# A ninth block pair by seven products, and the low parts of four down-projection weights made early and kept in DRAM

## The chip, the cores and the metric

The kernel runs on one core of one Trainium2 chip. TensorE (PE in the profile) multiplies matrices into PSUM, VectorE (DVE), ScalarE (ACT) and GpSimd (POOL) work on vectors, SyncE (SP) issues most of the transfers; ACT and POOL have transfer queues of their own. The metric is the time of one execution on the device, in microseconds, as the median of several runs.

## The reference, cut to what matters

One layer of a streaming encoder on 512 tokens of 1024 channels: four parallel token mixers with sigmoid gates and an output projection, a cross-attention into 256 memory tokens, and a gated MLP with a short causal convolution. The change touches the last gated mixer branch and the MLP:

```python
hf = _rms_norm(x, norm_ffn_pre[l])
u = _dwconv_causal(hf @ w_up[l], ffn_dw[l]) + ffn_dw_b[l]
u_g, u_v = jnp.split(u, 2, axis=-1)
yff = (jax.nn.silu(u_g) * u_v) @ w_down[l]
x = x + _rms_norm(yff, norm_ffn_post[l])
```

`w_up` is 1024 x 5632 (the first 2816 columns are the gate, the others the value), `w_down` is 2816 x 1024. Everything is float32.

## The kernel before, in words

**Number format.** A float32 matrix is held as a high part (a cast to the matmul type float32r) and a low part (the rest), and a product is three matmuls: high by high, high by low and low by high (`mm3`, line 245 in `matmul`). The split of a weight is a cast on ACT and a subtraction on DVE (`split_weights`, lines 202 and 203; `split_to`, lines 1673 and 1674). A weight of [128, 1024] is loaded into a raw tile (two of tag `wr`), split into a high and a low tile, and these come from four places each in turn (`weights_tile`, tags `wh0` to `wh3` and `wl0` to `wl3`). A new weight can be written into a place once every matmul on the weight four before it is done.

**Order.** All stages are one stream of jobs (`run_blocks`): a job has a load and split, done up to three jobs ahead, and a body with the matmuls. An entry without weights (`then`) only runs its body in its turn. The order within each engine is then settled by a planner of the tile framework: it runs through the instructions with durations of its own and takes, on each engine, what is ready there, with the program's order as priority. Semaphores hold the order between engines on the chip.

**The mixer's last branch** (`last_branch_jobs`): for the forgetting attention, eight gate blocks and four branch blocks, twelve weights of 512 KB, each with 24 matmuls of 512 columns. The output projection of the mixer comes next, by seven products in place of eight on half blocks (`SEVEN`), with sums of weights formed earlier and stored in DRAM (`Sums`).

**The up-projection** (`up_jobs`). The 22 blocks of 128 channels of gate and value are made block by block. Blocks 0 to 3 are plain. A plain block half is 24 matmuls of 512 columns. From block 5 on, every second block takes gate and value together as a 2 by 2 product of half blocks, by seven products of 12 matmuls of 256 columns each (`seven`), and the block before it is plain and laid between the products. These pairs go from 5 to 19 in the kernel before; blocks 20 and 21 are plain. In a pair, the bodies are: `a` (two products, weight: the gate block), `b` (two products, weight `z.s`, a sum of quarter blocks), `c` (one product, weight: the changed value block), `d` (one, weight `z.t`, half as wide) and `end` (one, again the weight of `c`). Between them stand the plain block's gate half (after `a`), the first half of its value (after `b`) and the second half of its value (after `d`, `second_half`, which still reads the weight fetched for the first). The sums of weights are made by POOL (lines 1755 to 1759). The sums of activations over the tokens' halves, which the products `b`, `c` and `end` read, are made once per call by `token_sums` on POOL (lines 1663 and 1665) and split into `tokh` and `tokl` (`token_split`). After the products, `done` adds the bias on ACT (line 1697) and the convolution's other taps on DVE (line 627), which frees the PSUM bank.

Beside this, in the pairs, POOL forms sums of `w_down` for the next stage (`ns.sums`, lines 575 to 578), and DVE forms sums of the activations of each pair of blocks (`down_sums`, lines 1684 to 1686).

**The down-projection** (`down_jobs`) again goes by seven products, on 11 pairs of blocks in two phases; phase 0 has two weights per pair, with 12 matmuls of 512 columns each (products M1 and M6, then M5 and M7). Its raw weights come on SP's queue (line 594) into `dw` tiles, three ahead, and are split by `split_to`. The products keep their sums in PSUM; the banks are named by tags `sc`, `tr`, `mm` and `av`, two banks each. Before, M1, M6, M5 and M7 had `sc`, `tr`, `mm` and `av`.

Of the kernel before, what the change touches and what calls it, by code (L numbers as in the profile page):

```python
# [25 lines left out]
P = 128  # L26
# [60 lines left out]
def hybrid_layer(ctx: ExitStack, tc: tile.TileContext, a: dict, out: bass.AP):  # L87
# [520 lines left out]
    def seven_banks(phase):  # L608
        names = (("M2", "sc"), ("M3", "tr"), ("M4", "mm")) if phase else (("M1", "sc"), ("M6", "tr"), ("M5", "mm"),
                                                                         ("M7", "av"))  # L610
        return {name: [bank(tag) for _ in range(2)] for name, tag in names}
# [756 lines left out]
    def last_branch_jobs():  # L1368
        yield then(open_last_branch)
        gf = gate_blocks(1, "f", mix_place, mix_done)  # L1370
        yield next(gf)
        yield next(gf)
        yield share("mm", "av")
        yield from gf
# [264 lines left out]
    def open_ffn():  # L1639
# [27 lines left out]
    def token_split(i):  # L1667
        hi, lo = ns.tok
        A.copy(hi[:, i], ns.quart[i - 4])
        V.tensor_tensor(lo[:, i], ns.quart[i - 4], hi.bitcast(F32)[:, i], ALU.subtract)  # L1670
# [17 lines left out]
    def up_jobs():  # L1688
# [56 lines left out]
        def seven(j):  # L1745
# [28 lines left out]
            def summed(i):  # L1774
                return [lambda k, h=h: h[:, i, k] for h in ns.tok]
# [39 lines left out]
        def early_places():  # L1815
            ns.pair_sums = []
            down_places(f"qa{NF // 2 - 1}", 2)

# [7 lines left out]
        pairs = {j: seven(j) for j in range(5, NF - 2, 2)}  # L1826
# [6 lines left out]
        for q, j in enumerate(pairs, EARLY - 1):  # L1833
# [37 lines left out]

        yield then(late_places)
        yield plain(NF - 2, 0, sums_of(3))
        yield plain(NF - 2, 1, sums_of(4))
# [239 lines left out]
```

## Time and profile before

| | |
|---|---|
| median of 3 runs | 1033.58 us (1033.11 to 1033.93) |
| profiled execution | 1035.12 us, of it span 1033.3 us |
| PE busy | 1024.4 us (99%), 5477 matmuls |
| DVE busy | 864.0 us (84%) |
| ACT busy | 534.4 us (52%) |
| POOL busy | 263.5 us (26%) |
| mean granted TensorE clock | 0.999 |

The span runs from the first to the last instruction of the profiled execution, and its own time is 1.8 us longer. A busy PE is one with a matmul in flight; the ends of matmuls are modelled and overlap, so the distance between starts is the better measure of a matmul's price. In a row of the chain or of the timeline the first number is the start in us from the span's start and the second the duration.

In the span, the mixer's last branch lies at about 497 to 562 us, the mixer's output from there to about 600, the up-projection's pairs from 733 to 905, the last plain blocks from there to 921, and the down-projection from 921 to 1027.

### The profile page before, as it was taken

How to read it: one execution, taken by the hardware profiler on the slowest of the kernel's cores; microseconds unless marked ns; L12 is line 12 of the kernel's file. 1: busy time of each engine (PE TensorE's matmuls, PEld its weight loads, DVE VectorE, ACT ScalarE, POOL GpSimd, SP SyncE). 2: the span in 40 equal slices, each digit the busy share in tenths (PEclk: the TensorE clock that was granted, in tenths of full speed). 3: DMA queues.
4: the chain of work that ended last, by engine and by line, in shares of the span. 5: the costliest groups of instructions: out<-in, count | busy, mean ns of one | idle time of the engine just before them, and what ended most of it. 6: DMA issues, size and time to landing. Idle time of an engine off the chain costs nothing.

```text
span 1033.3 us, 15189 instructions
## 1 busy us (share of the span) xinstructions
PE 1024.4 (99%) x5477; PEld 883.0 (85%) x5477; DVE 864.0 (84%) x1323; ACT 534.4 (52%) x893; POOL 263.5 (26%) x270
## 2 busy tenths in 40 slices
PE   9999999999999999999999999999999999999997
PEld 8888888888888988888888899999899899888886
DVE  7899999796878667888687898787989897799886
ACT  5322222376565466766543665655455455466662
POOL 4001000100011214442100031039177557226202
PEclk9999999999999999999999999999999999999999
DMA  7954344844434255767448834233456576626852
GB/s 248 317 176 106 104 147 143 280 143 115 141 102 140 63 157 137 195 184 188 154 146 264 262 123 123 82 97 116 134 164 209 180 225 210 197 81 187 274 161 82
DMA packets 194128, 169.40 MB, mean 164 GB/s; under 512 B 25295, under 2 KB 165692, under 8 KB 194053
## 3 DMA queue, kind: packets, MB, share of 16 engines
q1 hardware_dynamic: 187315, 145.08, 46.9%
q10 hardware_dynamic: 4178, 14.82, 3.9%
q0 software_dynamic: 2560, 8.54, 2.7%
q8 instruction: 43, 0.70, 0.3%
q14 instruction: 32, 0.26, 0.1%
HBM read 142.18 MB, written 26.23 MB: 163 GB/s over the span
## 4 chain that ended last, share of the span: by engine, by line
PE 95%; DVE 2%; DMA 1%; ACT 1%; issue 1%; POOL 0%; POOLq 0%; DVEq 0%; SPq 0%; ACTq 0%
PE ps_mm L245 41%; PE ps_av L245 26%; PE ps_tr L245 15%; PE ps_sc L245 11%; PE ps_tr L251 1%; PE ps_mm L463 1%; PE ps_av L463 1%; DVE e L860 0%; DMA xs<-in_x 0%; DMA ptl<-turned 0%; DVE e L1133 0%; DVE ptl L879 0%; ACT wh L202 0%; ACT e L1139 0%; DVE qk L820 0%
## 5 line engine op out<-in xcount | busy, mean ns | idle before, releaser
L202 ACT CAST wh<-wr 128x1024 fp32r<-128x1024 f32 (+1 forms) x124 | 129.5, 1046 | 188.6 <-PE ps_mm L245 70.4
L203 DVE TENSOR_TENSOR wl<-wr,wh 128x1024 fp32r<-128x1024 f32 (+1 forms) x124 | 165.3, 1334 | 30.0 <-ACT wh L202 29.5
L245 PE MATMUL ps_mm<-hth,wh 128*128 128x512 f32 (+1 forms) x472 | 173.5, 376 | 0.1
L245 PE MATMUL ps_mm<-htl,wh 128*128 128x512 f32 (+1 forms) x472 | 173.5, 376 | 0.0
L245 PE MATMUL ps_mm<-hth,wl 128*128 128x512 f32 (+1 forms) x472 | 173.2, 375 | 0.0
L245 PEld LDWEIGHTS ps_mm<-hth,wh 128*128 128x128 f32 x472 | 87.1, 188 | 15.7 <-ACT hth L164 0.3
L245 PEld LDWEIGHTS ps_mm<-hth,wl 128*128 128x128 f32 x472 | 87.0, 188 | 15.7
L245 PEld LDWEIGHTS ps_mm<-htl,wh 128*128 128x128 f32 x472 | 87.0, 188 | 15.2
L245 PE MATMUL ps_av<-htl,wh 128*128 128x512 f32 (+1 forms) x264 | 97.8, 370 | 0.0
L245 PE MATMUL ps_av<-hth,wh 128*128 128x512 f32 (+1 forms) x264 | 97.7, 370 | 0.0
L245 PE MATMUL ps_av<-hth,wl 128*128 128x512 f32 (+1 forms) x264 | 97.6, 370 | 0.0
L700 DVE SCALAR_TENSOR_TENSOR y<-y,par,y 128x508 f32<-128x508 f32 (+29 forms) x120 | 83.0, 733 | 0.0
L245 PEld LDWEIGHTS ps_av<-htl,wh 128*128 128x128 f32 x264 | 49.6, 188 | 8.1
L245 PEld LDWEIGHTS ps_av<-hth,wl 128*128 128x128 f32 x264 | 49.7, 188 | 8.0
L245 PEld LDWEIGHTS ps_av<-hth,wh 128*128 128x128 f32 x264 | 49.6, 188 | 8.0
L1673 ACT CAST wh<-dw 128x1024 fp32r<-128x1024 f32 x32 | 33.7, 1052 | 21.6 <-PE ps_av L245 8.1
L1674 DVE TENSOR_TENSOR wl<-dw,wh 128x1024 fp32r<-128x1024 f32 x32 | 39.6, 1243 | 5.5 <-ACT wh L1673 5.5
L245 PE MATMUL ps_tr<-htl,wh 128*128 128x512 f32 (+1 forms) x112 | 40.6, 363 | 0.0
L245 PE MATMUL ps_tr<-hth,wh 128*128 128x512 f32 (+1 forms) x112 | 40.6, 362 | 0.0
L245 PE MATMUL ps_tr<-hth,wl 128*128 128x512 f32 (+1 forms) x112 | 40.5, 361 | 0.0
L1920 POOL TENSOR_TENSOR qa<-qa 128x256 f32<-128x256 f32 x11 | 26.6, 2425 | 49.2 <-DVE wr L1674 25.2
L1127 POOL TENSOR_SCALAR fbias<-ck,cq 128x128 f32<-128x128 f32 (+3 forms) x32 | 21.3, 671 | 67.9 <-DVE st L1133 62.4
(558 smaller groups left out, 2739.1 us busy)
## 6 DMA issues: line engine op xcount, KB each, us to landing
wr<-in_w_in SPq DMA_DIRECT2D x38, 512.0 KB
wr<-in_w_gate SPq DMA_DIRECT2D x32, 512.0 KB
wr<-in_w_up SPq DMA_DIRECT2D x28, 512.0 KB
dw<-sums SPq DMA_DIRECT2D x44, 256.0 KB
wr<-in_w_branch SPq DMA_DIRECT2D x16, 512.0 KB
wq<-in_w_up SPq DMA_DIRECT2D x16, 512.0 KB
wp<-in_w_down ACTq DMA_DIRECT2D x14, 512.0 KB
sums<-wp ACTq DMA_DIRECT2D x14, 512.0 KB
```

The lines of the kernel that those rows point to most:

```text
L202: last_weights[:] = [order(A.copy(hi, raw[:, :n])).ins, low.tensor_tensor(lo, raw[:, :n], hi.bitcast(F32), ALU.subtract).ins]
L203: low.tensor_tensor(lo, raw[:, :n], hi.bitcast(F32), ALU.subtract).ins]
L245: steps_of[:] = [PE.matmul(ps, lhs, rhs, start=start, stop=stop, skip_group_check=again).ins]
L251: turns.append(PE.transpose(ps, x, ident[:n, :n]).ins)
L463: keep(PE.matmul(banks[c][:, :S // 2], w[p == 1][:, k, c * P:(c + 1) * P], ht[p == 2][:, i * 4 + k, :S // 2], start=(i, p, k) == (0, 0, 0) ...
L700: ins = V.scalar_tensor_tensor(dst[:, s:], src[:, :S - s], pc("conv_dw", k * 4 + j), dst[:, s:], ALU.mult, ALU.add)
L1127: G.tensor_scalar(bias[:, :w], ck[j][:, :w], -1.0, cq[:, qt, head:head + 1], ALU.mult, ALU.add)
L1673: A.copy(hi, x)
L1674: return V.tensor_tensor(lo, x, hi.bitcast(F32), ALU.subtract).ins
L1920: G.tensor_tensor(z[:, 1], z[:, 2], z[:, 1], ALU.subtract)
```

## The change

1. **Ninth pair.** The pairs go on to block 21, so blocks 20 and 21 become a pair with its plain block, as the eight before. Two plain halves (48 matmuls of 512 columns) become seven products (84 of 256).
2. **Places.** The split token sums become eight tiles of 4 KB per partition instead of two of 16 KB, so that each comes free by itself: the sums of activations for down go into four of them and into `z7` after body `c` of the last pair (`late_places`); three serve as raw tiles for down's second phase; and the last norm's gain, which was loaded as the up-projection opened, is loaded into one (`tokl3`) after the last product. The last pair of blocks has a tile of its own (`qlast`) in the place the gain had.
3. **Sums of activations.** `sums_of(2)` and `sums_of(3)` are issued after body `c` of the last pair, `sums_of(4)` after the held half of block 20, `sums_of(5)` after its last product.
4. **Banks.** In down M1, M6, M5, M7 have `mm`, `av`, `sc`, `tr` (and M2, M3, M4 have `mm`, `av`, `sc`), and the very last half product takes a `tr` bank.
5. **Low parts.** In the mixer's last branch four more jobs come after its second, fourth, eighth and tenth: each loads one of down's first four raw weights (two transfers of 256 KB on SP's queue), splits it as any weight, and stores the low part (512 KB) into a DRAM tile `lows` on POOL's queue. In down, the first four weights are cast on ACT as before, and their low parts are loaded from `lows` on POOL's queue instead of being subtracted on DVE.
6. **Start of the token sums.** A memset of one column of the first sum's tile on DVE is put behind the last norm before the MLP, and POOL's first token sum has to follow it.

```diff
     def last_branch_jobs():
         yield then(open_last_branch)
         gf = gate_blocks(1, "f", mix_place, mix_done)
-        yield next(gf)
-        yield next(gf)
-        yield share("mm", "av")
-        yield from gf
+        ns.lows = dram.tile([4 * P, D], F32R, name="lows")
+
+        def low_job(n):
+
+            def load():
+                raw = gp.tile([P, WB], F32, tag="wr", name="wr", bufs=2)[:, :D]
+                load_parts(raw, ns.sums.parts(0, n % 2, n // 2))
+                return split_weights(raw, [P, D])
+
+            return load, None, lambda hi, lo: G.dma_start(ns.lows[n * P:(n + 1) * P, :], lo) and None
+
+        for i, job in enumerate(gf):
+            if i == 2:
+                yield share("mm", "av")
+            yield job
+            if i in (1, 3, 7, 9):
+                yield low_job((1, 3, 7, 9).index(i))
...
-        ns.tok = [ns.fp.tile([P, 4, 4, S // 2], F32R, tag=n, name=n) for n in ("tokh", "tokl")]
-        ns.post = ns.fp.tile([P, D], F32, name="g_ffn")
+        ns.tok = [[ns.fp.tile([P, 4, S // 2], F32R, tag=f"{n}{i}", name=n) for i in range(4)] for n in ("tokh", "tokl")]
+        ns.last = ns.fp.tile([P, 4, S // 2], F32, name="qlast")
         ns.dw = {"dw": 1}
-        G.dma_start(ns.post, a["norm_ffn_post"][0].partition_broadcast(P))
...
+        with tc.issue_after(ns.normed[-1]):
+            V.memset(raw[0][:, 0, :1], 0.0)
...
+    def load_gain():
+        ns.post = ns.fp.tile([P, D], F32, tag="tokl3", name="g_ffn")
+        G.dma_start(ns.post, a["norm_ffn_post"][0].partition_broadcast(P))
...
-        pairs = {j: seven(j) for j in range(5, NF - 2, 2)}
+        def late_places():
+            for x in ("tokh0", "tokh1", "tokl0", "tokl1"):
+                down_places(x, 2)
+            down_places("z7", 1)
+
+        pairs = {j: seven(j) for j in range(5, NF, 2)}
...
-            if j == NF - 3:
-                yield then(lambda: down_places("z7", 2))
+            if j == NF - 1:
+                yield then(lambda: (late_places(), sums_of(2)(), sums_of(3)()))
             yield d
             yield then(lambda j=j, f=second_half: f(j - 1))
-            if j == NF - 3:
-                yield then(sums_of(2))
+            if j == NF - 1:
+                yield then(sums_of(4))
             yield e
+            if j == NF - 1:
+                yield then(load_gain)
             yield then(lambda q=q: add(q + 1))
-        def late_places():
-            down_places("tokh", NF // 2 - 4)
-            ns.quart[-1] = ns.fp.tile([P, 4, S // 2], F32, tag="tokl", name="qa")
-
-        yield then(late_places)
-        yield plain(NF - 2, 0, sums_of(3))
-        yield plain(NF - 2, 1, sums_of(4))
-        yield plain(NF - 1, 0, sums_of(5))
-        yield plain(NF - 1, 1)
+        yield then(sums_of(5))
...
-                if phase and len(raws) == 2 * pairs:
-                    parts["more"] = ns.fp.tile([P, 3, D], F32, tag="tokh", name="dw2")
                 k = (len(raws) - 2 * pairs) % 7
-                raw = parts["more"][:, k] if phase and k < 3 else dw_tile("dw")
+                raw = ns.fp.tile([P, D], F32, tag=f"tokh{k}", name="dw2") if phase and k < 3 else dw_tile("dw")
...
-            split_to(hi, lo, raw)
+            if n < 4:
+                A.copy(hi, raw)
+                G.dma_start(lo, ns.lows[n * P:(n + 1) * P, :])
+            else:
+                split_to(hi, lo, raw)
...
-                banks.update(seven_banks(phase))
+                banks.update(seven_banks(phase, ("mm", "av", "sc", "tr")))
```

More of the change, by code (lines that the diff above doesn't have):

```diff
@@ L606, in hybrid_layer, with seven_banks @@
              (1, 0): (("M2", 0), ("M3", 2)), (1, 1): (("M4", 1),)}
[L608 to L611, printed above, removed]
+    def seven_banks(phase, tags=("sc", "tr", "mm", "av")):
+        names = ("M2", "M3", "M4") if phase else ("M1", "M6", "M5", "M7")
+        return {name: [bank(tag) for _ in range(2)] for name, tag in zip(names, tags)}
     def y8(dtype=F32R):
@@ L1668, in token_split @@
         hi, lo = ns.tok
-        A.copy(hi[:, i], ns.quart[i - 4])
-        V.tensor_tensor(lo[:, i], ns.quart[i - 4], hi.bitcast(F32)[:, i], ALU.subtract)
+        split_to(hi[i], lo[i], ns.quart[i - 4])
     def split_to(hi, lo, x):
@@ L1774, in summed @@
             def summed(i):
-                return [lambda k, h=h: h[:, i, k] for h in ns.tok]
+                return [lambda k, h=h: h[i][:, k] for h in ns.tok]
             def body_a(*w):
@@ L1817, in early_places @@
             down_places(f"qa{NF // 2 - 1}", 2)
+            ns.quart[-1] = ns.last
         def splits(*which):
@@ L2018, in whole @@
                     cut = slice(c * S // pieces, (c + 1) * S // pieces)
-                    ps = bank("av") if c else None
+                    ps = bank("tr") if c else None
                     for q, job, ws in held:
```

## The prediction

> **What bounds the kernel now.** I read the page first, then TensorE's waits, then the busy times by stage, then the chain of waits around the code that changes.
>
> ```profile
> span 1033.3 us, 15189 instructions
> ...
> PE 1024.4 (99%) x5477; PEld 883.0 (85%) x5477; DVE 864.0 (84%) x1323; ACT 534.4 (52%) x893; POOL 263.5 (26%) x270
> ```
>
> ```profile
> PE ps_mm L404 <- DVE e L354: 1.3, 1, 1.3
> PE ps_av L245 <- DVE ptl L879: 0.4, 1, 0.4
> PE ps_tr L447 <- DVE nt L442: 0.2, 1, 0.2
> ```
>
> TensorE (PE) works through the whole span, and all its waits in the second view come to 1.9 us. None of them lies in the stages that change: the mixer's last branch, the up-projection and the down-projection have no PE wait. So time is won only where PE gets less to do, and lost where a matmul comes to wait.
>
> ```profile
> 884.00:905.00 21.00, 21.00 (x123) 18.56 (x122) 14.58 (x20) 8.53 (x13) 1.34 (x2) 1.00 0.56 178
> 905.00:916.00 11.00, 11.00 (x51) 9.09 (x49) 11.00 (x18) 5.98 (x9) 1.66 (x1) 1.00 0.21 60
> 916.00:927.00 11.00, 11.00 (x49) 9.02 (x48) 9.79 (x16) 7.29 (x13) 2.20 (x2) 1.00 0.40 130
> 927.00:940.00 13.00, 13.00 (x59) 10.70 (x58) 13.00 (x21) 7.91 (x11) 11.46 (x3) 1.00 0.41 121
> ```
>
> The columns after the length are busy PE, weight loads, DVE, ACT and POOL, then the granted clock, DMA share and GB/s. VectorE (DVE) is full from 905 to 940, over the last four plain blocks and the head of down, yet PE never stands still: DVE's queue is late there, but not late enough to be felt.
>
> **The ninth pair.** The chain gives the price of a block.
>
> ```profile
> 733.25 1.42 PE ps_tr L245 x12
> ...
> 905.05 5.44 PE ps_av L245 x24
> 910.49 5.44 PE ps_mm L245 x24
> 915.93 5.44 PE ps_av L245 x24
> ```
>
> ```profile
> 896.10 1.37 PE ps_sc L245 x12
> ...
> 899.99 1.42 PE ps_tr L245 x12
> ...
> 921.37 1.39 PE ps_sc L245 x6
> ```
>
> A plain block is 24 matmuls of 512 columns in 5.44 us, 0.2267 us each. From 733.25, the first product of the first pair, to 905.05, the start of the second-last block's value half, lie eight pairs and one plain block: 8 x 48 + 24 = 408 wide matmuls and 8 x 84 = 672 of 256 columns. 171.80 us less 408 x 0.2267 = 92.48 leaves 79.32, so 0.1180 us for a narrow one. The change takes 48 wide matmuls away (10.88 us) and adds 84 narrow ones (9.92): **-0.96 us**. By the quickest twelve shown (1.37 us) the 84 take 9.59, by the slowest (1.42) 9.94, so the bounds are -1.29 and -0.94.
>
> DVE, ACT and POOL pay for it:
>
> ```profile
> L1674 DVE TENSOR_TENSOR wl<-dw,wh 128x1024 fp32r<-128x1024 f32 x32 | 39.6, 1243 | 5.5 <-ACT wh L1673 5.5
> ```
>
> ```profile
> 889.43 0.69 DVE L203 TENSOR_TENSOR wl<-s,wh 128x512 fp32r<-128x512 f32 x1 [1.06 <-ACT wh L202]
> ```
>
> ```profile
> L1786 DVE TENSOR_TENSOR ps_sc<-ps_sc,mu 128x256 f32<-128x256 f32 x2 | 0.8, 416 | 0.0
> ```
>
> Instead of two weight splits the block has three and a half: on DVE one more of 1.24 and one of 0.69, and three adds of 0.42, +3.2 us. The low parts that leave down's head are four of 1.24, -5.0 us. DVE's total falls by 1.8 us while PE's falls by 0.96. The added work falls where a pair ends, a stage in which DVE was busy 14.58 of 21 us (the window from 884), so the 6.4 us free there cover it; uncovered it would cost at most its own 3.2 less the 5.0 that leave. I price it at nothing. POOL's four sums come after the last sums of down's weights and have POOL to themselves.
>
> **Down's first weights lose their lead.** This is where I expect something back. High and low parts go round in four places each; down's first four reuse the places of the four weights before them.
>
> ```profile
> 905.59 1.04 ACT L1673 CAST wh<-dw 128x1024 fp32r<-128x1024 f32 x1
> ...
> 910.30 1.06 ACT L1673 CAST wh<-dw 128x1024 fp32r<-128x1024 f32 x1 [1.95 <-PE ps_av L245]
> ...
> 915.74 1.06 ACT L1673 CAST wh<-dw 128x1024 fp32r<-128x1024 f32 x1 [2.66 <-PE ps_mm L245]
> ...
> 921.18 1.05 ACT L1673 CAST wh<-dw 128x1024 fp32r<-128x1024 f32 x1 [3.71 <-PE ps_av L245]
> ```
>
> Before, a place came free every 5.44 us: the second weight was cast at 910.30 for a use at about 921.37 + 12 x 0.2267 = 924.1. After, with E the end of the last product, the tail is the third product (1.42), the fourth (1.37), the held half of block 20 (12 x 0.2267 = 2.72) and the last product (1.42). The second weight takes the place that the held half reads, free at E - 1.42; the third takes the place that the last product reads, free at E. Their low parts are now loads on POOL's queue that can't be issued earlier.
>
> ```profile
> L1402 POOL DMA_DIRECT2D xin<-in_x x4: 527/562/595, 562.0 to 612.5; - x4
> ...
> DMA to landing us min/median/max: 3.6/4.9/6.8
> ```
>
> ```profile
> g_ffn<-in_norm_ffn_post POOLq DMA_DIRECT2D x1, 512.0 KB, 5.2
> ```
>
> Loads of the same 512 KB on the same queue landed in 3.6 to 6.8 us. The second weight's low part is there at E - 1.42 + 4.9 = E + 3.48; PE wants it at its second matmul, E + 2.72 + 0.23 = E + 2.95. That is a wait of **0.53 us**, between 0 (3.6 us) and 2.43 (6.8 us). I take the median's: the DMA share there, 0.40, is moderate. The third lands at E + 4.9, plus some 0.6 for the gain's issue that now stands before it on POOL, against E + 5.67: in time. The fourth's place is free before the third's. The Trainium skill, "DMA: Bandwidth & Descriptors", section "Anatomy of one DMA — SWDGE (gpsimd) path", fits such a transfer by 2.0 us and its bytes at 436 GB/s, an estimate of 3.2 us here; by that nothing would wait and the change would be worth -0.96. The trace disagrees (no x load under 3.6), so the measured times decide.
>
> **The copies in the last branch.**
>
> ```profile
> 505.00:521.00 16.00, 16.00 (x80) 13.51 (x79) 9.22 (x14) 9.06 (x14) 1.30 (x3) 1.00 0.37 126
> ...
> 535.00:550.00 15.00, 15.00 (x68) 12.42 (x67) 13.16 (x17) 6.52 (x9) 1.87 (x4) 1.00 0.67 217
> 550.00:556.00 6.00, 6.00 (x28) 4.99 (x27) 0.38 (x3) 1.05 (x1) 0.00 (x0) 1.00 0.72 236
> ```
>
> ```profile
> 517.52 2.00 ACT L202 CAST wh<-wr 128x1024 fp32r<-128x1024 f32 x2 [4.47 <-PE ps_av L245]
> ```
>
> ```profile
> 559.88 2.54 DVE L165 TENSOR_TENSOR wl<-wr,wh 128x1024 fp32r<-128x1024 f32 x2
> ```
>
> ```profile
> 564.63 1.36 PE ps_mm L245 x6
> ```
>
> Four times a 512 KB load in two pieces on SP's queue, a cast of some 1.0 us, a subtraction of about 1.24 and a 512 KB store on POOL's queue. The weights run ahead of PE here until their places are full (ACT stood 4.47 us for PE), and DVE and DMA have room in the first and third window of these, so I price this at nothing. The tightest successor is the second weight of the mixer's output, split by about 562.4 and used at 564.63: 2.2 us spare. If the last copy came straight before it, 1.24 of DVE and 512 KB at 217 GB/s (2.4 us) would overrun this by 1.4 us; that is the upper bound. The stores precede the memory tokens' loads on POOL and may hold them; PE needs the memory only after the mixer's output.
>
> **The rest.**
>
> ```profile
> 696.38 1.29 DVE L300 SCALAR_TENSOR_TENSOR nt<-res,st_r,g_pre 128x1024 f32<-128x1024 f32 x1 [0.91 <-POOL st_r L290]
> ```
>
> ```profile
> 697.09 9.88 POOL L1663 TENSOR_TENSOR qa<-hth,htl 128x1024 f32<-128x1024 f32 x4
> ```
>
> ```profile
> 729.86 1.22 DVE L1670 TENSOR_TENSOR tokl<-qa,tokh 128x1024 fp32r<-128x1024 f32 x1
> ```
>
> ```profile
> 741.55 1.41 PE ps_tr L245 x12
> ```
>
> ```profile
> L1986 DVE TENSOR_TENSOR o<-o,g_ffn x2: 686/686/687, 989.6 to 990.2; 128x512 f32<-128x512 f32 x2
> ```
>
> The one-column memset holds the token sums until the last norm's product ends, 697.67 instead of 697.09. Their second split ended at 731.1 for a use at 741.55: 10 us of cover. The output gain's load goes from the start of up to its end and is used near 989.6, some 69 us later. The banks only change names; the one that the last block frees late was av and is now tr. Nothing for these.
>
> **Sum.** -0.96 + 0.53 = -0.43. Against the profiled execution (1035.12 us with a span of 1033.35, 1.5 us above the median) that is 1034.7; against the median of 1033.58 it is **1033.1 us**.
>
> **Rivals.** (1) POOL's queue is held up by the full DVE: slower.
>
> ```profile
> 562.00:571.00 9.00, 9.00 (x41) 7.48 (x40) 8.83 (x14) 5.39 (x6) 1.03 (x2) 1.00 0.92 305
> ```
>
> ```profile
> 927.79 1.12 POOL L1920 TENSOR_TENSOR qa<-qa 128x256 f32<-128x256 f32 x1 [0.74 <-DVE hth L1674]
> 929.71 13.99 POOL L1920 TENSOR_TENSOR qa<-qa 128x256 f32<-128x256 f32 x3 [0.80 <-DVE htl L1674]
> ```
>
> At down's head POOL's subtraction grew from 1.12 to 13.99 / 3 = 4.66 us beside a full DVE. Were each POOL load late by the same 3.54, the second low part would come 0.53 + 3.54 = 4.1 us late and the third, 3.54 behind it on the queue, at about E - 1.42 + 8.44 + 3.54 = E + 10.6 against E + 5.67 + 4.1 = E + 9.7: another 0.8. Then +4.9 - 0.96 = +3.9, 1037.5. It decides from a wait of 3.0 us. Against it: two x loads were issued at 562, where DVE was busy 8.83 of 9 us, and no x load took over 6.8. The Trainium skill, "SBUF — State Buffer", section "SBUF: two separate sides", speaks for it: a vector instruction that holds the port shared with GpSimd keeps GpSimd from writing a DMA's descriptors. The stretched subtractions agree that something is shared; the x loads don't show it for descriptors. (2) The low parts come in time, or PE's planned order has other matmuls first (at 921.37 it already goes bank by bank), and the narrow matmuls run at their quickest: -1.29, 1032.3. (3) The last copy holds the mixer's output: +1.4 - 0.43, 1034.5. (4) The new order moves the narrow matmuls of all pairs to their quickest: 672 x (0.1180 - 0.1142) = 2.6 more, with -1.29: 1029.7. Only single rows speak for it; each of the twelves shown but one took 1.41 or 1.42.
>
> **How the numbers follow.** Forecast 0.55 (by the bounds of the load and of the narrow matmuls 1033.58 - 1.29 = 1032.3 to 1033.58 - 0.94 + 2.43 = 1035.1), rival 1 0.16, rival 2 0.17, rival 3 0.07, rival 4 0.05. A measurement can tell 0.2%, 2.1 us, from no change. Faster by that: rival 4 and a little of 2, 0.07. Slower by that: rival 1 and the worst of 3, 0.18. Within: 0.75. The range 1031.6 to 1036.2 holds the forecast, 2, 3 and the mild half of 1.
>
> **What would show it.** Four 512-column matmuls' worth of PE time less (96 narrow halves become 84 narrow products) before down begins; a PE wait of about half a microsecond for a DMA into wl in the second job of down; POOL loads of lows landing in 3.6 to 6.8 us; no PE wait near 564; DVE no longer full from 927 to 940. A PE wait of 3 us or more there, or any in the last branch, would make the forecast wrong, as would a pair's product at another price than 9.9 us.

## The result, and the profile after

The changed kernel takes **1051.55 us** (median of four runs, 1050.7 to 1052.02), the kernel before, run beside it, 1033.64 us (1033.11 to 1033.93): a ratio of **1.0173**, 95% interval 1.0155 to 1.0191. It is 17.9 us slower; 1033.1 had been predicted, in a range up to 1036.2. The head of the page of the changed kernel, and its chain of waits by engine:

```profile
span 1049.9 us, 15300 instructions
...
PE 1026.3 (98%) x5513; PEld 884.9 (84%) x5513; DVE 863.8 (82%) x1329; ACT 540.9 (52%) x902; POOL 268.6 (26%) x282
...
PE 87%; DMA 6%; DVE 2%; issue 2%; ACT 1%; POOL 1%; POOLq 0%; SPq 0%; DVEq 0%; ACTq 0%
```

PE's part of the chain that ended last fell from 95% to 87%; transfers now have 6% of it, where they had 1%. TensorE's waits after (engine, tile and line, what it waited for: us in total, times, longest):

```profile
PE ps_mm L245 <- DVE ge L1187: 6.2, 1, 6.2
PE ps_sc L245 <- DMA wl<-lows: 2.3, 2, 1.9
PE ps_mm L245 <- DMA wl<-lows: 1.8, 1, 1.8
...
PE ps_tr L251 <- DVE qa L1673: 1.3, 1, 1.3
PE ps_av L245 <- DVE wl L203: 1.0, 1, 1.0
PE ps_mm L245 <- ACT ge L1175: 0.9, 1, 0.9
```

Three places are new: the last branch and the mixer's output behind it (the first row and the last two), the last norm before the MLP (`qa`), and the head of down (`lows`). Summed over the starts of all matmuls, the time beyond 0.2267 us for 512 columns (0.1133 for 256, other widths in proportion) grew from 32.6 to 50.6 us, by 17.9: 12.0 of it between 540 and 580 us, 1.1 at 508, 1.5 at 711 and 5.0 from 930 to 945, with small changes of both signs elsewhere. Against that stands 1.36 us less work by the same prices; together this is the 16.6 us between the two spans (1049.9 and 1033.3 us).

**The mixer's output.** PE's rows there, with the 6.22 us it stood still:

```profile
567.60 0.39 PE L245 MATMUL ps_mm<-wh,mix 128*128 128x512 f32 x1
574.21 0.79 PE L245 MATMUL ps_mm<-wh,mix 128*128 128x512 f32 x1 [6.22 <-DVE ge L1187]
```

The releaser named is a row of DVE, `ge`, that reads a product of the branch. The chain of the changed kernel tells why it was late (start, duration, what; lines are left out):

```profile
523.63 4.05 DMA wr<-in_w_gate
...
527.76 1.06 ACT wh L202
...
528.84 1.24 DVE wl L203
...
530.09 3.75 DMA wr<-in_w_branch
```

```profile
564.88 6.27 DMA wr<-out_sums
...
571.25 1.05 ACT wh L164
...
572.33 1.23 DVE wl L165
573.56 0.61 DVE ge L1187
```

Every weight goes through one of two raw tiles, and the next load into a tile can only go out when the cast and the subtraction of the weight before are done: 4.05 + 1.06 + 1.24 us, then the next load at 530.09. The copies' loads take turns in the same two tiles. At the end of the chain the third weight of the mixer's output is loaded at 564.88, cast at 571.25 and subtracted at 572.33; on DVE `ge` stands behind that subtraction, and PE waits for the bank it empties. What PE was about to multiply, the second weight, had been split since 565.83; only the bank was missing. And `ge` could have run earlier: the row of ACT that it needs ended at 562.27, and DVE stood idle for 6.50 us before the subtraction. With `ge` first, PE would have come to the third weight after nine matmuls (2.0 us) and found its low part at 573.56; as it was, it used that at 577.36. So some 4 us of the loss are the order on DVE, an estimate from these rows that no run tests. In the kernel before, the same cast began 11 us earlier:

```profile
560.12 1.03 ACT L164 CAST wh<-wr 128x1024 fp32r<-128x1024 f32 x1
```

**The norm.** DVE and POOL after, and POOL before:

```profile
707.90 3.41 DVE L300 SCALAR_TENSOR_TENSOR nt<-res,st_r,g_pre 128x1024 f32<-128x1024 f32 x1 [0.92 <-POOL st_r L290]
```

```profile
707.83 2.40 POOL L1676 TENSOR_TENSOR qa<-hth,htl 128x1024 f32<-128x1024 f32 x1
```

```profile
696.48 0.59 POOL L1650 DMA_DIRECT2D g_ffn<-in_norm_ffn_post  x1
```

The norm's product took 1.29 us before and takes 3.41 now: POOL's first token sum started 0.07 us ahead of it. Before, the issue of the gain's load stood in POOL's way for 0.59 us, so the norm went first; the change moved that load. The memset holds the first sum of the program, but the planner puts another sum first, which it doesn't hold.

**The head of down.** POOL's rows, and busy times from 930 (length, PE, weight loads, DVE, ACT, POOL, clock, DMA share, GB/s):

```profile
926.18 0.59 POOL L1957 DMA_DIRECT2D wl<-lows  x1 [9.78 <-PE ps_sc L245]
930.59 0.53 POOL L1957 DMA_DIRECT2D wl<-lows  x1 [3.81 <-DVE ps_tr L1813]
932.41 0.53 POOL L1957 DMA_DIRECT2D wl<-lows  x1 [1.29 <-PE ps_sc L245]
935.30 0.53 POOL L1694 DMA_DIRECT2D g_ffn<-in_norm_ffn_post  x1 [2.36 <-PE ps_tr L245]
935.82 0.54 POOL L1957 DMA_DIRECT2D wl<-lows  x1
```

```profile
930.00:945.00 15.00, 10.95 (x58) 8.53 (x57) 14.26 (x27) 9.86 (x15) 9.18 (x8) 1.00 0.93 335
```

PE waited at 938.1, 940.2 and 944.1 for the second, third and fourth low part, each 7.5 to 8.2 us after its issue. The DMA engines were 0.93 busy, where the row of before had 0.40. The fourth part's place comes free only with PE's last product of the up-projection, as the gain's does, whose issue stands ahead of it.

### The profile page after: what moved, and what is told of

Read it like the earlier page. It is cut to its first block, busy times and chain, and to the rows that moved or that the text cites. A ratio compares the mean times of both kernels' runs of the same rounds, so it can differ in the third digit from the quotient of the medians.

```text
span 1049.9 us, 15300 instructions
## 1 busy us (share of the span) xinstructions
PE 1026.3 (98%) x5513; PEld 884.9 (84%) x5513; DVE 863.8 (82%) x1329; ACT 540.9 (52%) x902; POOL 268.6 (26%) x282
## 4 chain that ended last, share of the span: by engine, by line
PE 87%; DMA 6%; DVE 2%; issue 2%; ACT 1%; POOL 1%; POOLq 0%; SPq 0%; DVEq 0%; ACTq 0%
PE ps_mm L245 37%; PE ps_av L245 23%; PE ps_tr L245 14%; PE ps_sc L245 11%; DMA wr<-in_w_gate 2%; PE ps_tr L251 1%; DMA wr<-out_sums 1%; DVE wl L203 1%; DMA wr<-in_w_branch 1%; DMA wl<-lows 1%; DMA wr<-sums 1%; ACT wh L202 1%; PE ps_mm L463 1%; PE ps_av L463 1%; DMA wr<-in_w_up 0%
## 5 line engine op out<-in xcount | busy, mean ns | idle before, releaser
L245 PE MATMUL ps_mm<-hth,wh 128*128 128x512 f32 (+1 forms) x464 | 170.5, 376 | 0.9 <-ACT ge L1175 0.9
L245 PE MATMUL ps_mm<-htl,wh 128*128 128x512 f32 (+1 forms) x464 | 170.5, 376 | 0.0
L245 PE MATMUL ps_mm<-hth,wl 128*128 128x512 f32 (+1 forms) x464 | 170.1, 375 | 0.0
L245 PE MATMUL ps_av<-hth,wl 128*128 128x512 f32 (+1 forms) x256 | 94.6, 370 | 1.0 <-DVE wl L203 1.0
L245 PE MATMUL ps_av<-htl,wh 128*128 128x512 f32 (+1 forms) x256 | 94.6, 370 | 0.0
L245 PE MATMUL ps_av<-hth,wh 128*128 128x512 f32 (+1 forms) x256 | 94.5, 369 | 0.0
L1686 DVE TENSOR_TENSOR wl<-dw,wh 128x1024 fp32r<-128x1024 f32 x28 | 34.4, 1235 | 8.0 <-ACT wh L1685 8.0
L1685 ACT CAST wh<-dw 128x1024 fp32r<-128x1024 f32 x28 | 29.4, 1054 | 17.2 <-PE ps_av L245 11.8
L287 POOL TENSOR_TENSOR st_m<-pm,nhalf 128x1 f32<-128x1 f32 x12 | 5.4, 453 | 109.3 <-ACT junk L1478 44.1
```

What stands on the lines that cost most here:

```text
L245: steps_of[:] = [PE.matmul(ps, lhs, rhs, start=start, stop=stop, skip_group_check=again).ins]
L287: G.tensor_tensor(m, parts[0], eps[:, :n], ALU.add)
L1685: A.copy(hi, x)
L1686: return V.tensor_tensor(lo, x, hi.bitcast(F32), ALU.subtract).ins
```

## The experiments

All times are set beside runs of the kernel before on the same chip at the same time. e1 is the median of four runs and e12 of eleven; each of the others is one run.

| run | us | minus before |
|---|---|---|
| e1 pair alone | 1037.32 | +4.25 |
| e2 copies alone | 1044.67 | +11.60 |
| e3 copies without stores | 1041.61 | +8.54 |
| e4 stores alone | 1033.12 | +0.05 |
| e5 copies, raw tiles of their own | 1041.34 | +8.52 |
| e6 e1, both sums held | 1037.57 | +4.75 |
| e7 e1, sums later | 1035.54 | +2.72 |
| e8 change, gain later | 1049.07 | +16.25 |
| e9 e5, memory's load held | 1036.07 | +3.23 |
| e10 loads only | 1033.13 | +0.29 |
| e11 splits only | 1032.77 | -0.07 |
| e12 e1, e6 and a longer e7 | 1032.69 | -0.15 |
| e13 e9 without stores | 1033.05 | -0.10 |
| e14 change, lows on SP | 1048.99 | +15.84 |
| e15 change, gain on SP | 1048.41 | +15.26 |
| e16 change, e6, e9 and e15 | 1037.27 | +4.12 |

The four runs of e1 lay between 1036.4 and 1039.04, so differences of a microsecond between the others are read from the waits, not from the times.

### The parts one by one: e1 to e4

e1 is the changed kernel without the four copies, and with DVE's subtraction in down as before:

```diff
-        for i, job in enumerate(gf):
-            ...
-            if i in (1, 3, 7, 9):
-                yield low_job((1, 3, 7, 9).index(i))
+        yield next(gf)
+        yield next(gf)
+        yield share("mm", "av")
+        yield from gf
...
-            if n < 4:
-                A.copy(hi, raw)
-                G.dma_start(lo, ns.lows[n * P:(n + 1) * P, :])
-            else:
-                split_to(hi, lo, raw)
+            split_to(hi, lo, raw)
```

> The ninth pair and the freed tiles stay; the four copies in the last branch, their stores and their loads in down are left out, and down's first four low parts are subtracted on DVE as before. If the copies are the loss (they hold the last branch by some 12 us and their loads hold down's head by some 5), the time falls from 1051.5 to near the forecast without them: 1033.6 - 0.96 + 1.5 (the norm held at about 709) = 1034.1, and no PE wait is left between 500 and 600. If the pair itself is the loss (its banks and its splits at down's head), it stays above 1038 with PE waits for DVE or ACT near 925 to 945.

The ratio is 1.0046, 95% interval 1.0029 to 1.0063; the time is above the 1034.1 us of the first case and under the 1038 of the second, so both have a part. TensorE's waits of e1, and the DVE rows ahead of the longest:

```profile
PE ps_mm L245 <- DVE wl L1673: 3.2, 1, 3.2
...
PE ps_tr L251 <- DVE qa L1660: 1.1, 1, 1.1
```

```profile
925.16 0.68 DVE L1673 TENSOR_TENSOR htl<-pairs,htl 128x512 fp32r<-128x512 f32 x1
925.76 0.74 DVE L626 SCALAR_TENSOR_TENSOR c<-ps_sc,par,c 128x510 f32<-128x510 f32 x1
...
927.35 0.42 DVE L1688 TENSOR_TENSOR pairs<-qa 128x256 f32<-128x256 f32 x1
927.68 1.22 DVE L1673 TENSOR_TENSOR wl<-dw,wh 128x1024 fp32r<-128x1024 f32 x1
```

So the pair alone already loses: the norm's wait is there, and at the head of down a weight cast at 923.47 is subtracted only at 927.68, behind activations' splits, a tap and sums of activations. e2 is the kernel before with the four copies and their stores alone (the `low_job` lines of the change, nothing in down); e3 leaves out the stores; e4 has no copies, but stores four low parts that the branch forms anyway.

```diff
-            return load, None, lambda hi, lo: G.dma_start(ns.lows[n * P:(n + 1) * P, :], lo) and None
+            return load, None, lambda hi, lo: None
```

> The kernel before with only the four copies added to the last branch and their low parts stored, which nothing reads (down splits as before, eight pairs, no memset). If the copies cost the last branch what the trace of after shows there, the time is 1033.6 + 12 to 13 = 1046, with PE waits between 540 and 580 of some 10 us. If the loss there needs the pair or the later planning, it is within 2 us of 1033.6.

> The same copies with no store: four more raw weights loaded and split in the last branch, and nothing kept. Theory ring: the two raw tiles and the transfers into them bound the weights, one turn of a raw tile being a load of 4 to 7 us, a cast of 1.0 and a subtraction of 1.2; then this alone costs 8 us or more, about 1042 to 1046. Theory POOL order: the stores stand in front of the memory tokens' loads on POOL's queue, and ACT waits in order for these; then this costs 2 us or less, about 1034 to 1036.

> The stores without the loads and splits: four low parts that the last branch has anyway (of its own weights, with the same places in the order) are stored to DRAM on POOL's queue, and nothing reads them. Theory POOL order: the first memory load is issued at about 510 instead of 505, ACT stands for it, and some 3 us or more are lost, 1037 or above. Theory ring: nothing is lost, 1033 to 1035, since no raw tile turns more often.

The first row of TensorE's waits in e2:

```profile
PE ps_mm L245 <- DVE ge L1188: 6.5, 1, 6.5
```

The copies alone cost 11.6 us, 8.5 of it without a store, at the same place as in the changed kernel. Stores on POOL's queue, two of them ahead of the memory's loads, cost nothing by themselves (e4).

### Which resource of the copies: e5, e9, e10, e11, e13

e5 gives the copies raw tiles of their own, in space that the keys of the memory take later, and puts the first of them behind the branch's fourth job instead of its second, the second behind the sixth instead of the fourth:

```diff
-                raw = gp.tile([P, WB], F32, tag="wr", name="wr", bufs=2)[:, :D]
+                raw = ns.xm.tile([P, D], F32, tag=("kxh", "kxl")[n % 2], name="lr")
...
-            if i in (1, 3, 7, 9):
+            if i in (3, 5, 7, 9):
```

> The kernel before plus the four copies with their stores, as in e2, but the copies' raw weights are loaded into two tiles of their own (in space that this stage leaves free) and no longer take turns in the two raw tiles of the branch; the copies stand after jobs 4, 6, 8 and 10. Same loads, casts, subtractions and stores as e2. Theory A (the loss is the two raw tiles: each turn of load, cast and subtraction goes round them, four more turns use up the lead): the cost falls from +11.6 us to at most 3, so 1033 to 1036.5 us, and TensorE's 6.5 us wait at the mixer's output falls under 2 us. Theory B (the loss is the transfers' share or the in-order queues of ScalarE, VectorE and GpSimd, which carry the same work here): the cost stays at 8 us or more, 1041 us or above, with the 6 us wait still there.

At 1041.34 us the time spoke for theory B, but the waits had moved:

```profile
PE ps_av L245 <- DVE e L1159: 2.5, 1, 2.5
PE ps_mm L245 <- DVE ge L1188: 1.6, 1, 1.6
```

The 2.5 us lie at 500 us, ahead of any copy. With the keys' tiles gone from there, the memory's loads had lost what held them:

```profile
493.23 0.57 POOL L1286 DMA_DIRECT2D g_mem<-in_norm_mem  x1 [1.09 <-PE ps_sc L245]
```

In the kernel before this load goes out at 504.41, and that of the memory's tokens right behind it, as here. 1 MB more ran beside a round trip through DRAM, whose write took this long in e5's chain:

```profile
496.25 7.32 DMA turned<-e
```

In the kernel before, the read behind the same write went out 2.5 us after it (498.42 and 500.89). The early loads were an effect of the edit, so e9 reserves the two tiles where the keys' were, and changes nothing else:

```diff
-        ns.kx = (ns.xm.tile([P, 4, MEM], F32R, name="kxh"), ns.xm.tile([P, 4, MEM], F32R, name="kxl"))
+        ns.lr = [ns.xm.tile([P, D], F32, tag=t, name="lr") for t in ("kxh", "kxl")]
...
+                raw = ns.lr[n] if n < 2 else ns.xm.tile([P, D], F32, tag=("kxh", "kxl")[n % 2], name="lr")
```

> As e5 (the kernel before plus four copies with stores, raw weights in two tiles of their own), but these tiles are reserved where the key tiles were, so that the loads of the memory tokens are held until 504 us as in the kernel before; in e5 they went out at 493 and a round trip through DRAM (half of the scores) came 4 us late. Theory A (two raw tiles were the main cost of the copies, and e5's early loss was only this displaced load): no wait near 500, the cost is what e5 lost at the mixer's output, 3 to 4.5 us, so 1036 to 1037.5. Theory B (the copies' transfers and engine work cost 8 us wherever their raw tiles are): 1041 us or more, the wait comes back at the mixer's output.

1036.07 us: of the copies' 11.6 us 3.2 are left, as theory A had it, and of the waits at the mixer's output these:

```profile
PE ps_mm L245 <- DVE ge L1188: 1.4, 1, 1.4
...
PE ps_mm L245 <- DVE wl L165: 0.7, 1, 0.7
```

e10, e11 and e13 take e9 apart. The first two edits are e10's and e11's; e13 has e3's.

```diff
-                return split_weights(raw, [P, D])
+                return raw,
```

```diff
+        for t in ns.lr:
+            V.memset(t, 0.5)
...
-                load_parts(raw, ns.sums.parts(0, n % 2, n // 2))
-                return split_weights(raw, [P, D])
+                return split_weights(ns.lr[n % 2], [P, D])
```

> As e9, but the four copies only load their raw weight (2 MB in all) into the tiles of their own; no cast, no subtraction, no store. Theory T (what is left after e9 is the transfers: more bytes on the same engines make the weights' loads land later): at least half of e9's cost stays, 2 us or more, 1035 or above. Theory E (it is the casts and subtractions in order on ScalarE and VectorE, and the turns in the four places of high and low parts): the cost is under 0.7 us, 1033.5 or less.

> As e9, but the four copies load nothing and store nothing: they cast and subtract a tile that was filled once, into the places of the weights' high and low parts. Theory E (casts, subtractions and the turns in the places): 2 us or more of cost, 1035 or above, with a TensorE wait at the mixer's output. Theory T (the transfers): under 0.7 us, 1033.5 or less.

> As e9, but the four low parts are not stored; loads, casts and subtractions stay. Theory A (what is left of e9's 3.2 us is the four stores of 512 KB): 1033.0 to 1033.8 us and no TensorE wait at the mixer's output. Theory B (it is loads, casts and subtractions together, which alone cost nothing in e10 and e11): 1035 us or more, the wait of 1.4 us still there.

Loads alone +0.29 us, splits alone -0.07, loads and splits together -0.10: nothing, so neither theory of e10 and e11 held, and theory A of e13 did. So the 2 MB, the four casts and subtractions and the turns in the places of the high and low parts are hidden, as had been predicted; what they cost is the passage through the two raw tiles (e3 against e13: 8.6 us), and with the stores another 3 (e9 against e13: 3.3, e2 against e3: 3.1), while stores without copies are free (e4). One thing stands beside the tiles in the first of these: the first two copies also come later in e13 than in e3. What that move is worth alone wasn't tried; of e3's loss 1.2 us lie at 508 us, near these two, and 7.6 at the mixer's output, behind the two copies that stayed where they were. TensorE's waits of e13 in full:

```profile
PE ps_tr L447 <- DVE nt L442: 1.4, 1, 1.4
PE ps_mm L404 <- DVE e L354: 1.3, 1, 1.3
```

Whether a store costs by its bytes or by its place on POOL's queue wasn't told apart; in e9's profile no instruction waits for a store to land. e4 doesn't settle it, since its last store goes out at 532.10 us and that of e9 at 547.62, nearer to the loads of the mixer's output.

### The pair's own loss: e6, e7, e12

e6 holds the sum that the planner puts first as well; e7 takes sums of activations out of the head of down; e12 has the first and a longer form of the second.

```diff
             V.memset(raw[0][:, 0, :1], 0.0)
+            V.memset(raw[3][:, 0, :1], 0.0)
```

```diff
-                yield then(lambda: (late_places(), sums_of(2)(), sums_of(3)()))
+                yield then(lambda: (late_places(), sums_of(2)()))
...
-                if 6 <= q + 2 < pairs:
-                    down_sums(q + 2, low)
+                for k in ((3, 4) if q == 2 else (q + 2,) if 5 <= q + 2 < pairs else ()):
+                    down_sums(k, low)
```

`sums_of(4)` and `sums_of(5)` go too; in e12 the last lines are `if 3 <= q + 1 < pairs: down_sums(q + 1, low)`.

> As e1 (the pair without copies and low parts) plus one more one-column memset behind the last norm, on the tile of the fourth token sum, which the planner puts first and which the change's memset doesn't hold. Theory A (GpSimd's first token sum, started just before the norm's two-input product on VectorE, makes that 3.4 us instead of 1.29): the product is back at about 1.3 us, TensorE's wait for it (0.8 us in e1) falls to 0.2 and its wait for the sums' parts too; the time is 1.0 to 1.5 us under e1, about 1036.0. Theory B (the hold itself costs, since token sums come later): the time is e1's or more, 1037.3 to 1038.5, with a longer wait for the token parts in the first pair.

> As e1, but three of the sums of activations (the fourth, fifth and sixth pair's), which VectorE makes between the last pair's products and the head of down, are made in down's own turns two or three pairs ahead of their use. Theory A (at down's head TensorE waits 3.2 us for the subtraction of a weight that stands behind the activations' splits, the convolution's taps and these sums in VectorE's full queue): the wait falls to 1 us or less and the time by 2.0 to 3.5 us, to 1033.8 to 1035.3. Theory B (it is the places: the weight's low part can't be written before the product that reads the place ends): the wait stays at 2.5 us or more and the time within 0.8 us of e1's 1037.3.

> The ninth pair without copies and low parts, both first token sums held behind the norm (e6), and the sums of activations from the fourth pair on made in down's own turns, one pair ahead of their use. Theory A (the pair's own loss is the norm beside GpSimd and VectorE's queue at down's head, and both can be ordered away): the 1.3 us at the norm and most of the 2 us that e7 still lost at down's head are gone and the seven products' gain of about 1.3 us shows: 1032 to 1033.2 us, a ratio to before of 0.999 to 1.000. Theory B (VectorE stays the limit at down's head whatever the order): 1 us or more stays there, 1034 us or above, ratio over 1.001.

In e6 the norm is back at its old price and PE's wait for `qa` is gone:

```profile
694.74 1.28 DVE L300 SCALAR_TENSOR_TENSOR nt<-res,st_r,g_pre 128x1024 f32<-128x1024 f32 x1 [0.91 <-POOL st_r L290]
```

That is theory A for the place, though the time didn't fall: by matmul starts this run lost 0.8 us more in its first 15 us and 1.3 more at the head of down than e1 did. The 1.3 are clock and not order: after the same wait of 3.2 us e6's next matmuls started 0.43 us apart and e1's didn't (rows in the last section). In e7 the wait at the head fell from 3.2 to 1.1 us and the time by 1.8 (1.5 beside its own run of before), both a little short of theory A's figures and far from theory B's, so most of it was the order of DVE's queue. Of e12's waits:

```profile
PE ps_mm L245 <- DVE wl L1674: 0.4, 1, 0.4
```

This wait is left at the head, 0.7 us by matmul starts, and nothing at the norm. e12 takes 1032.69 us against 1032.84, a ratio of 0.9999, interval 0.9990 to 1.0009: nearly all of the pair's loss can be ordered away. The 0.96 us that its products should save would be a ratio of 0.9991, just inside the interval, and the 0.7 at the head takes most of it back, so the runs neither show nor exclude the gain. No version here is faster than the kernel before by more than the noise.

### Why the low parts come late: e8, e14, e15, e16

e8 meant to load the gain later; the planner put it ahead of the fourth low part again (932.11 against 932.63), so it tells nothing of theory A or B, and its 1049.07 us is the changed kernel's order once more. Its 2.5 us under the changed kernel's time lie at the mixer's output, where less was lost (9.4 us in place of 12.0 by matmul starts), in code that is the same. e14 loads the low parts on SP's queue, e15 only the gain.

```diff
-                G.dma_start(lo, ns.lows[n * P:(n + 1) * P, :])
+                SP.dma_start(lo.bitcast(F32), ns.lows[n * P:(n + 1) * P, :].bitcast(F32))
```

```diff
-        G.dma_start(ns.post, a["norm_ffn_post"][0].partition_broadcast(P))
+        SP.dma_start(ns.post, a["norm_ffn_post"][0].partition_broadcast(P))
```

> As the changed kernel, but the output gain is loaded during down's ninth job instead of ahead of the fourth low part. Theory A (the fourth low part's load stands on GpSimd's queue behind the gain's, which has to wait for TensorE's last product of the up-projection, and shares its time with it): the load is issued 1 us or more earlier, TensorE's waits for low parts (2.3 and 1.8 us) fall to 2.5 us together or less, and the time by 1.5 to 2.5 us, to about 1049.5. Theory B (the loads land late through the busy DMA engines alone, 0.93 in that stretch): the low parts still land in 6 to 8 us, the waits stay above 3.3 us together and the time within 0.8 us of 1051.5.

> As the changed kernel, but the four low parts come back on SyncE's queue (the same bytes, seen as float32), the gain stays on GpSimd's. Theory A (the loads land in 6 to 8 us since the DMA engines are 0.93 busy there): they still land late, TensorE's waits for low parts stay above 3 us together and the time is 1050 us or more. Theory B (GpSimd's queue is late, by its order behind the gain and beside a full VectorE): the waits fall under 1.5 us together and the time to 1048 to 1049.5.

> As the changed kernel, but the output gain is loaded on SyncE's queue, so that the fourth low part isn't behind it on GpSimd's; this is what e8 meant to do, where the planner had put the gain ahead again. Theory A (the fourth low part is late by its place behind the gain, which waits for TensorE's last product): its load goes out 2 us or more earlier, TensorE's last wait for a low part (1.8 us) is gone and the time falls by 1.5 to 2.5 us, to 1049 to 1050. Theory B (the transfers alone): the waits and the time stay as they are, within 0.8 us of 1051.5.

The profile has the landing of a load on POOL's queue. In the changed kernel the four low parts took 3.9, 7.5, 7.8 and 8.2 us from issue to landing; the median:

```profile
wl<-lows POOLq DMA_DIRECT2D x4, 512.0 KB, 7.6
```

For SP's queue it has none, so PE's rows must tell. In e14 the loads were issued at 923.10, 927.50, 929.33 and 932.33, and PE waited for the third and the fourth:

```profile
937.16 0.50 PE L245 MATMUL ps_sc<-wl,hth 128*128 128x512 f32 x1 [2.32 <-DMA wl<-lows]
...
940.89 0.50 PE L245 MATMUL ps_mm<-wl,hth 128*128 128x512 f32 x1 [1.63 <-DMA wl<-lows]
```

These two were there 7.8 and 8.6 us after their issue, as late as on POOL's queue. The second was not: PE started on it 5.8 us after its issue, where it had taken 7.5. The waits, 2.3 and 1.6 us, are theory A's figure. The time, 1048.99 us, is theory B's, but e8, with the changed kernel's order, took 1049.07, so the waits decide: for the third and the fourth part POOL's queue isn't the cause, for the second it may have a share. In e15 the fourth load goes out as soon as its place is free:

```profile
932.24 0.53 POOL L1957 DMA_DIRECT2D wl<-lows  x1 [2.47 <-PE ps_tr L245]
```

That is half a microsecond earlier than behind the gain, not the 2 us of theory A. PE's last wait fell from 1.8 to 0.7 us, and another rose from 1.9 to 2.4. The time fell by 3.1 us, more than theory A had it, but 2.7 of these lie at the mixer's output, which the edit doesn't touch. By matmul starts from 905 to 960 us, where the kernel before loses 0.2, the head lost 5.5 us in the changed kernel, 5.9 in e8, 5.0 in e14 and 4.7 in e15: queue and order are worth about a microsecond at most, and the rest goes with transfers that land late in a stretch full of them. That these transfers come down to 4.9 us if fewer run beside them wasn't tried.

e16 is the whole change with the edits of e6, e9 and e15 shown above.

> The whole change with the copies' raw weights in tiles of their own (as e9), both first token sums held (as e6) and the gain on SyncE's queue (as e15). If the costs found one by one add up: 1051.5 less 8.5 (ring), 1.3 (norm) and 1.5 to 2.5 (gain) gives 1039 to 1040.5; the low parts' loads at down's head still cost about 3 us and the stores about 3. If they overlap or something else is at work: 1043 us or more, or under 1037.

1037.27 us, under the 1039 to 1040.5 worked out and 0.27 above the bound under which something else would have been at work. The longest of TensorE's waits in e16:

```profile
PE ps_sc L245 <- DMA wl<-lows: 2.0, 1, 2.0
```

By matmul starts 4.7 us are lost at the head, of them some 1.5 in matmuls that started 0.43 us apart after this wait, and 1.0 at the mixer's output, where e9 lost 2.7. The parts don't quite add up: with the stores in it, the mixer's output gave back more than e9 had promised, and why wasn't tried.

## Why the prediction was wrong, step by step

**The copies in the last branch, priced at nothing.** This is the step that failed most: 11.6 us alone (e2). It named the right work, and found cover for each engine and for the transfers; e10, e11 and e13 bear that out. It missed the resource that all of it passes through. "The weights run ahead of PE here until their places are full" is true of the four places of high and low parts, but a weight needs a raw tile first, and there are two. By the chain a turn takes 4.05 + 1.06 + 1.24 = 6.35 us, so with two tiles a copy uses up at least 3.2 us of the lead and the four 12.7. That is an estimate; without stores the copies cost 8.5 us through these tiles (e3), and how much the branch's slack took up wasn't measured. The 2.2 us spare were read for the second weight of the mixer's output, at 562.4, where the third's subtraction ends; the third, with a bank read on DVE behind its subtraction, was the one that broke. Rival 3 had the right place (564) and asked only what the last copy overruns, 1.4 us: it counted one copy where the lead of four was gone.

**Down's first weights, +0.53 us.** The mechanism was right, PE does wait for loads into `wl`, but the terms were mis-sized. With E at about 935, the second load went out at E - 4.4 and the third at E - 2.5, both earlier than the prediction's E - 1.42 and E; but they and the fourth took 7.5 to 8.2 us in place of 4.9, more than the 6.8 of the upper bound. The DMA share that stood beside the choice of the median, 0.40, was that of a stretch without these loads; with them it is 0.93. The x loads that gave the median were of two kinds in the kernel before. The two issued at 562, into the stretch whose DMA share the prediction shows as 0.92:

```profile
DMA to landing us min/median/max: 6.0/6.4/6.8
```

The two issued at 605 and 613 (DMA share 0.75 from 604 to 609 and 0.31 from 612 to 617):

```profile
DMA to landing us min/median/max: 3.6/3.7/3.8
```

The busy pair was the nearer case, and its rows were there to be read. That the third lands in time and that "the fourth's place is free before the third's" both failed: it is the fourth that takes the place of the last product. 4.1 us of waits for `lows` came of it, of the size that rival 1 gave (4.1 for the second and 0.8 for the third), but for the third and fourth not by its mechanism: on a queue that POOL has no part in (e14) they are as late, and only the second came 1.7 us sooner there. (The 4.66 us that rival 1 took for a stretched subtraction was the mean of 11.16, 1.73 and 1.18.) The fit that the prediction cites from the Trainium skill, "DMA: Bandwidth & Descriptors", section "Anatomy of one DMA — SWDGE (gpsimd) path", gives 3.2 us here; the first load took 3.9, the three after it, in the stretch at 0.93, 7.5 to 8.2. The rule that it cites from the Trainium skill, "SBUF — State Buffer", section "SBUF: two separate sides", descriptors held back by DVE, isn't seen in the third and the fourth load; the 1.7 us of the second leave it open.

**DVE's work of the pair, priced at nothing.** Wrong by the 3.2 us wait of e1, which the changed kernel doesn't have, since the low parts don't pass DVE there. The total was no trouble (DVE has 863.8 us busy after, 864.0 before); the order was not looked at. In the last stretch before down, splits, taps and sums stand in one queue, and one weight's subtraction comes behind them. e7 and e12 show it by moving the sums. DVE also stays nearly full from 930 (14.26 of 15 us), which the prediction had denied.

**The memset, the gain and the sums' start, priced at nothing.** Wrong by 1.3 us: 10 us of cover for the sums themselves, but the norm beside them grew from 1.29 to 3.41 us, and is back at 1.28 when both sums are held (e6). By the rows, the gain's issue, 0.59 us on POOL ahead of the sum, was the cover that the change took away: an issue that seemed to cost nothing had kept two engines apart.

**The ninth pair, -0.96 us.** The count is right: 8 matmuls of 512 columns less in each group of rows.

```profile
L245 PE MATMUL ps_mm<-hth,wh 128*128 128x512 f32 x400 | 156.3, 391 | 0.9 <-ACT ge L1175 0.9
```

```profile
L245 PE MATMUL ps_mm<-hth,wh 128*128 128x512 f32 x408 | 159.4, 391 | 0.1
```

The first is of the changed kernel, the second of before; over the six groups (`ps_mm` and `ps_av`) 48 less, and 5513 matmuls for 5477 is 84 narrow ones more. At e12's time the gain can't be seen or denied. Rivals 2 and 4 didn't come up.

## What to carry to other kernels

Before work is added to a stage "with room", list what each piece passes through besides the engines: raw tiles, places, banks, and its position in every in-order queue; divide the time of a turn by the number of tiles to estimate how much lead a piece uses up, and follow the lead to the stage after. Price a load by the transfers that will run beside it after the change, not by those of before. When a small instruction is moved, look at what it kept apart.

## What the runs showed of the hardware that had not been expected

After the 6.22 us in which PE stood still its matmuls of 512 columns started 0.43 us apart until 579.49, in place of 0.2267, which lost another 2.6 us (twelve starts in 5.28 us), and the granted clock shows it (two rows of the changed kernel; the third figure from the end):

```profile
562.00:575.00 13.00, 6.23 (x25) 4.56 (x24) 5.99 (x7) 4.94 (x6) 1.05 (x2) 0.91 0.75 246
575.00:590.00 15.00, 15.00 (x59) 12.14 (x58) 12.66 (x15) 7.98 (x9) 0.00 (x0) 0.85 0.72 230
```

In e2, after 6.50 us, this ended already at 576.70, after 3.6 us. And after the wait of 3.2 us at the head of down the clock stayed whole in e1 (first row) and halved in e6 (second row):

```profile
928.00:931.00 3.00, 2.05 (x9) 1.70 (x10) 3.00 (x5) 0.09 (x1) 3.00 (x3) 1.00 0.51 182
```

```profile
928.00:931.00 3.00, 2.39 (x6) 1.91 (x7) 3.00 (x5) 0.44 (x1) 3.00 (x3) 0.51 0.54 156
```

So a wait of PE can have a price behind it, up to 2.6 us here, and waits of the same length cost more in one run than in another. The Trainium skill, "TensorE: Matmul & The Clock Gate", section "Part 1: The HAM clock gate", says that the array falls to half its clock after an idle window and needs some 3.4 us of work to come back; the half rate agrees, and the 5.3 us here are longer.

DVE's product with two SBUF operands and POOL's addition didn't share: started 0.07 us after POOL's 2.40 us, it took 3.41 us, its own 1.29 and nearly all of the other's. The Trainium skill, "SBUF — State Buffer", section "SBUF: two separate sides", has the shared port pair as a lock that the first to start holds for its whole instruction; the rows agree.
